# Seven products for more K pairs of a float32 feed-forward, with weight sums on GpSimd

## The chip, the cores and the metric

One core of one Trainium2 chip runs the whole program. The metric is the device time of one execution in microseconds (us), the median of three runs. TensorE (PE) multiplies, VectorE (DVE) and ScalarE (ACT) prepare its operands and read its results, GpSimd (POOL) adds, SyncE (SP) issues the loads.

## The reference, cut to what matters

Two transformer blocks in float32 over 256 tokens of width 2048. Only the matrix products of the two feed-forward networks and the residual around them are touched:

```python
# first block: silu(gate) * up, D_FF = 5632
x = x + (jax.nn.silu(h @ w_gate[l]) * (h @ w_up[l])) @ w_down[l]
# second block: a causal width-3 convolution between the products
u = causal_dwconv(jnp.einsum('bsd,df->bsf', h2, w_up[l]), conv_w[l], conv_b[l])
x = x + jnp.einsum('bsf,fd->bsd', jax.nn.silu(u_gate) * u_val, w_down[l])
```

## The kernel before, in words

**Float32 by three products.** An operand is cut into a high half (float32 rounded to the fp32r type) and a low half (the difference). `split` (L78) does it for weights: ACT casts a loaded tile `raw` into `wh` (L80), DVE subtracts `wh` from `raw` into `wl` (L81). `mm3` (L131) then issues high x high, high x low, low x high, three matmuls of 512 columns into one PSUM bank (L132 to L134). `wh` and `wl` have four buffers of 1024 columns each.

**The large products.** `gemm` (L167) makes 256 tokens x 1024 columns, four PSUM banks, over `nk` K pairs (a pair is 2 x 128 rows of K, one 1 MB load). A plain pair needs 8 `mm3`, that is 24 matmuls. For the first `n_sum` pairs Winograd's form of Strassen's scheme is used: 7 products of sums, 21 matmuls. It needs sums of the activations (`Pair.sums`, four 128-column blocks, made once per pair on POOL at L122 to L125) and sums of the weight blocks, `ta` and `tb`, made on DVE for every tile (L187 to L189). Each such pair has four cuts: 512 columns of `raw`, 1024 of `ta`, 1024 of `raw`, 1024 of `tb`. After the last of them a chain of five operations (L212 to L216) turns the seven sums into corrections `plus`, which are added to the banks at the end (`block` L243, `add_blocks` L253 on POOL and L254 on DVE).

**Where it is called.** FFN1: 11 gate/up gemms with `nk` = 8 ("gates" below), in three parts of 3, 4 and 4; after each part two down gemms (`g` = 0, 1) over 6, 8 and 8 pairs. FFN2: `conv` (L917) makes one 128-row block at a time with the weights as the moving operand; after each part two down gemms over 6, 8 and 8 pairs. Two pairs of each gate and each down are sevens (`N_SUM` = `N_SUMD` = 2). The products of the first block's attention output, of the second block's gates and of its output projection use `gemm` with no seven.

**Order.** The program text gives dependencies and priority; a scheduler that works with its own timing model fixes the order of each engine's queue at compile time, and each engine then runs its queue in that order. Loads go through SP's queue into three `raw` buffers of 2048 columns.

**Between the stages.** The residual and the constants are loaded in the first projections (`consts`, four loads one behind another). Before FFN2 the row norm is finished (`rtok_from` L315, `bcast` L350): sums on DVE, a square root on ACT, a diagonal `dg` on DVE, one matmul by PE (L355), a copy by ACT. The first `conv` stands behind it.

Of the kernel before, what the change touches and what calls it, by code (L numbers as in the profile page):

```python
# [17 lines left out]
P = 128  # L18
# [12 lines left out]
N_SUM = 2  # L31
N_SUMD = 2
TT_BUFS = 1
# [21 lines left out]
def body(ctx: ExitStack, tc: tile.TileContext, xT, xn, gfr, gp, cst, rst, w1, wo1, wgu, wd,  # L55
# [6 lines left out]
    rp = ctx.enter_context(tc.tile_pool(name="rp", bufs=3))  # L62
# [25 lines left out]
    class Pair:  # L88
# [29 lines left out]
        def sums(self, stag, v):  # L118

            f = sx.tile([P, 4, P], F32, tag="sf", name="sf", bufs=2)  # L120
            a11, a12, a21, a22 = v[:, 0, 0:P], v[:, 1, 0:P], v[:, 0, P:S], v[:, 1, P:S]
            pool.tensor_sub(f[:, 0], a21, a22)  # L122
            pool.tensor_sub(f[:, 2], a11, a21)
            pool.tensor_sub(f[:, 1], f[:, 0], a11)
            pool.tensor_add(f[:, 3], a12, f[:, 1])  # L125
            s = sx.tile([P, 2, 4, P], F32R, tag=stag, name=stag)
            act.copy(s[:, 0], f)
            dve.tensor_sub(s[:, 1], f, s[:, 0].bitcast(F32))
            self.s = s
# [10 lines left out]
    def wstat(ps, src, xs, first=True, last=True):  # L140
        raw = raw_tile(src)
        n = 2 * len(xs)
        h = (n + 1) // 2
        for a, b in ((0, h), (h, n)):
            wh, wl = split(raw[:, a * P:b * P], (b - a) * P)
            for k in range(a, b):
                o = (k - a) * P
                mm_w(ps, wh[:, o:o + P], wl[:, o:o + P], xs[k // 2], k % 2,
                     first and k == 0, last and k == n - 1)

    def xstat(src4, xr, pre=(), then=None):
        pp = (bank("d"), bank("d"))
        for q in range(4):
            raw = pre[q] if q < len(pre) else raw_tile(src4[q])
            if then and q in then:
                then[q]()
            for h, kn in ((0, 1), (1, 1), (2, 2)) if pre and q == 0 else ((0, 2), (2, 2)):
                wh, wl = split(raw[:, h * 512:(h + kn) * 512], kn * 512)
# [8 lines left out]
    def gemm(srcs, xs, n_sum, mid=None, tag="d"):  # L167


        nk = len(xs)  # L170
        plus = None
        if n_sum:
            p1, p5, p7 = bank(), bank(), bank()
            c = [[bank("d"), bank("d")], [None, None]]
            p6 = bank()
            c[1] = [bank("d"), bank("d")]
            p2, p3, p4 = c[0][0], c[0][1], c[1][0]
        else:
            c = [[bank(tag), bank(tag)], [bank(tag), bank(tag)]]
        for i in range(n_sum):  # L180
            st, sp_ = i == 0, i == n_sum - 1
            raw = raw_tile(srcs[i])
            b11, b12, b21, b22 = (raw[:, o:o + 512] for o in (0, 512, 1024, 1536))
            ta = sx.tile([P, 2, 512], F32, tag="ta", name="ta", bufs=TT_BUFS)
            tb = sx.tile([P, 2, 512], F32, tag="tb", name="tb", bufs=TT_BUFS)
            b1122 = raw.rearrange("p (a b) -> p a b", b=512)[:, 0:4:3, :]
            dve.tensor_add(ta, b1122, b12.unsqueeze(1).to_broadcast([P, 2, 512]))  # L187
            dve.tensor_add(tb[:, 0], ta[:, 0], b22)
            dve.tensor_add(tb[:, 1], tb[:, 0], b21)  # L189
            pr = xs[i]  # L190
            s = pr.s

            def S_(q):
                return s[:, 0, q], s[:, 1, q]

            def A_(j, t):
                return pr.a(0, j, t), pr.a(1, j, t)

            wh, wl = split(b11, 512)
            mm3(p1, *A_(0, 0), wh[:, 0:512], wl[:, 0:512], st, sp_)  # L200
            wh, wl = split(ta.rearrange("p a b -> p (a b)"), 1024)
            mm3(p5, *S_(0), wh[:, 0:512], wl[:, 0:512], st, sp_)
            mm3(p7, *S_(2), wh[:, 512:1024], wl[:, 512:1024], st, sp_)
            wh, wl = split(raw[:, 1024:2048], 1024)
            mm3(p2, *A_(1, 0), wh[:, 0:512], wl[:, 0:512], st, False)
            mm3(p3, *S_(3), wh[:, 512:1024], wl[:, 512:1024], st, False)
            wh, wl = split(tb.rearrange("p a b -> p (a b)"), 1024)
            mm3(p6, *S_(1), wh[:, 0:512], wl[:, 0:512], st, sp_)
            mm3(p4, *A_(1, 1), wh[:, 512:1024], wl[:, 512:1024], st, False)
        if n_sum:  # L210
# [6 lines left out]
            plus = [[s1, u4], [u3, e22]]  # L217
        for i in range(n_sum, nk):
            raw = raw_tile(srcs[i])
            ws = [split(raw[:, j * 1024:(j + 1) * 1024], 1024) for j in range(2)]  # L220
            order = [(j, t, n) for j in range(2) for t in range(2) for n in range(2)]
            if i == nk - 1:
                order = [(j, t, n) for t in range(2) for n in range(2) for j in range(2)]
            for j, t, n in order:
                wh, wl = ws[j]
                o = n * 512
                mm3(c[t][n], xs[i].a(0, j, t), xs[i].a(1, j, t), wh[:, o:o + 512], wl[:, o:o + 512],
                    i == n_sum and j == 0 and (n_sum == 0 or (t == 1 and n == 1)), i == nk - 1 and j == 1)
            if mid and i == min(n_sum + 1, nk - 1):
                mid()  # L230
        return c, plus

    ET_BUFS = 10
# [32 lines left out]
    def pair_of(srcs, i, tag, gains=None, stag=None, pool_=xp):  # L266
# [8 lines left out]
        else:  # L275
            v = sx.tile([P, 2, S], F32, tag="sv", name="sv", bufs=2)
# [97 lines left out]
    raw0 = rp.tile([P, 2048], F32, tag="raw", name="raw")  # L374
    for a, b in ((0, 1), (1, 2), (2, 4), (4, 8), (8, 12), (12, 16)):
        lo = 0 if a == 0 else 16 + a * S
        nc.sync.dma_start(xin[:, lo:16 + b * S], xT[:, lo:16 + b * S])
        if b <= 4:
            nc.sync.dma_start(raw0[:, a * 512:b * 512], w1[0][0][:, a * 512:b * 512])
# [4 lines left out]
        if b == 4:  # L384
            first.append(raw0)
        elif a in (4, 8):
            first.append(raw_tile(w1[0][a // 4]))
# [10 lines left out]
    with tc.tile_pool(name="a1", bufs=1) as ap1:  # L398
# [13 lines left out]
        def consts():  # L412
            for d, src in ((cst_t, cst), (rst_t, rst), (gp_t, gp), (resid, xn)):
# [117 lines left out]
        for grp in range(4):  # L531
# [38 lines left out]
    sx = sctx.enter_context(tc.tile_pool(name="sx", bufs=max(1, N_SUM)))  # L570
# [12 lines left out]
    for part, (ga, gb) in enumerate(PARTS):  # L583
        n_pairs = 2 * (gb - ga)
        hs = [None] * n_pairs
        for gi in range(ga, gb):
            c, p = gemm(wgu[gi], xr, N_SUM, run_late)
            ht = []
            for t in range(2):
                gt = et("gt")  # L590
                act.activation(gt, block(c, p, t, 0), AF.Silu, scale=rt[:, t:t + 1])
                h = et("h")
                dve.scalar_tensor_tensor(h, block(c, p, t, 1), rt[:, t:t + 1], gt, op0=ALU.mult, op1=ALU.mult)
# [7 lines left out]
        for g in range(2):  # L601
            c, p = gemm([wd[g][2 * ga + i] for i in range(n_pairs)], hs, N_SUMD, run_late)
# [6 lines left out]
    for g, n in enumerate(("ta", "tb")):  # L609
        gf.append(sx.tile([P, 2, 512], F32, tag=n, name="gf", bufs=TT_BUFS))  # L610
# [257 lines left out]
    sx = sctx.enter_context(tc.tile_pool(name="sy", bufs=max(1, N_SUM)))  # L868
    mr = [None] * 8
    ET_BUFS = 6  # L870
    with tc.tile_pool(name="mg", bufs=8) as mp:
        for b in range(4):
            c, p = gemm(wgs[b], xr, 0, run_late)
            gs = [[None, None], [None, None]]
            for t in range(2):
                for n in range(2):
                    gs[t][n] = mp.tile([P, 512], F32, tag="gs", name="gs")
# [28 lines left out]
        for g in range(2):  # L906
            c, p = gemm(wo2[g], mr, N_SUMW, run_late)
# [3 lines left out]
        rt = rtok_from(sq_done(), "rtok", EPS)  # L911
        rb = bcast(rt, "rb")
# [158 lines left out]
```

## Time and profile before

| | |
|---|---|
| median of 3 runs | 2578.12 us (2577.94 to 2578.13) |
| the profiled execution | 2575.72 us, of it the span 2573.8 us |
| mean granted TensorE clock | 0.995 |
| PE busy | 2530.7 us (98%) |
| DVE busy | 1821.8 us (71%) |
| ACT busy | 1340.8 us (52%) |
| POOL busy | 167.3 us (7%) |

The span runs from the first to the last instruction. A matmul's busy time overlaps that of the next one, so the distance between the starts of two matmuls, not the duration of one, says what a matmul costs. A duration of DVE or POOL in these rows runs from the instruction's start to its end, so it holds any time in which it was held up after its start.

### The profile page before, as it was taken

The numbers are of one execution on the slowest core, as the hardware profiler recorded it, in microseconds if no ns is written. First come the engines' busy times: TensorE is split into PE (matmuls) and PEld (weight loads), VectorE is DVE, ScalarE is ACT, GpSimd is POOL, SyncE is SP. The second block draws the span as 40 slices with busy tenths as digits, with TensorE's granted clock in tenths as the row PEclk, the third lists the DMA queues.
The fourth block names the chain that finished last, engine by engine and source line by source line (L and its number), as shares of the span: only waits on it lengthen the run. The fifth ranks groups of instructions, "written<-read, shape, count | busy, mean of one in ns | idle before, by whom it ended". The sixth has DMA issues, their size and how long they took to land. (4 is left out here: it accounts for less than half of the span.)

```text
span 2573.8 us, 31105 instructions
## 1 busy us (share of the span) xinstructions
PE 2530.7 (98%) x12050; PEld 2094.5 (81%) x12050; DVE 1821.8 (71%) x2354; ACT 1340.8 (52%) x1882; POOL 167.3 (7%) x125
## 2 busy tenths in 40 slices
PE   7999999999999999999999999999899999999999
PEld 6888887878878888777888888888788888888887
DVE  6666556789778877877566555455589887878796
ACT  4555555555555454546455644444455455545553
POOL 3000000102101100110000000000000100110011
PEclk9999999999999999999999999999999999999999
DMA  7444444545545555554544455555455655555554
GB/s 273 152 158 170 171 164 158 190 176 198 209 167 210 180 210 170 197 196 165 195 161 154 176 180 188 189 195 180 154 190 180 210 183 185 192 196 184 193 178 166
DMA packets 66244, 472.60 MB, mean 184 GB/s; under 512 B 7345, under 2 KB 7601, under 8 KB 9777
## 3 DMA queue, kind: packets, MB, share of 16 engines
q1 hardware_dynamic: 65520, 468.53, 51.8%
q8 instruction: 94, 1.54, 0.2%
q10 hardware_dynamic: 576, 2.10, 0.2%
q14 instruction: 54, 0.43, 0.0%
HBM read 468.50 MB, written 2.10 MB: 183 GB/s over the span
## 5 line engine op out<-in xcount | busy, mean ns | idle before, releaser
L81 DVE TENSOR_TENSOR wl<-raw,wh 128x1024 fp32r<-128x1024 f32 (+1 forms) x882 | 1082.4, 1234 | 597.3 <-ACT wh L80 596.1
L80 ACT CAST wh<-raw 128x1024 fp32r<-128x1024 f32 (+1 forms) x882 | 902.0, 1029 | 995.1 <-PE d L134 649.5
L133 PE MATMUL d<-wl,x 128*128 128x512 f32 x1532 | 599.6, 393 | 11.6 <-DVE wl L81 11.6
L134 PE MATMUL d<-wh,x 128*128 128x512 f32 x1532 | 597.9, 392 | 0.0
L132 PE MATMUL d<-wh,x 128*128 128x512 f32 x1532 | 572.1, 394 | 3.4 <-ACT wh L80 3.2
L137 PE MATMUL a<-x,wh 128*128 128x512 f32 x1536 | 542.0, 398 | 0.0
L138 PE MATMUL a<-x,wl 128*128 128x256 f32 x1536 | 431.6, 281 | 0.0
L133 PEld LDWEIGHTS d<-wl,x 128*128 128x128 f32 x1532 | 288.4, 188 | 74.8 <-DVE wl L81 15.2
L137 PEld LDWEIGHTS a<-x,wh 128*128 128x128 f32 x1536 | 289.0, 188 | 70.1
L132 PEld LDWEIGHTS d<-wh,x 128*128 128x128 f32 x1532 | 287.1, 188 | 67.1 <-ACT wh L80 8.2
L134 PEld LDWEIGHTS d<-wh,x 128*128 128x128 f32 x1532 | 288.6, 188 | 59.1 <-DVE x L116 0.5
L138 PEld LDWEIGHTS a<-x,wl 128*128 128x128 f32 x1536 | 290.9, 189 | 0.2
L133 PE MATMUL d<-wl,y 128*128 128x512 f32 x624 | 242.2, 391 | 0.0
L134 PE MATMUL d<-wh,y 128*128 128x512 f32 x624 | 241.5, 390 | 0.0
L132 PE MATMUL d<-wh,y 128*128 128x512 f32 x624 | 217.3, 392 | 0.1
L133 PEld LDWEIGHTS d<-wl,y 128*128 128x128 f32 x624 | 117.1, 188 | 27.0 <-DVE wl L81 2.3
L132 PEld LDWEIGHTS d<-wh,y 128*128 128x128 f32 x624 | 116.5, 188 | 25.8 <-ACT wh L80 2.2
L134 PEld LDWEIGHTS d<-wh,y 128*128 128x128 f32 x624 | 117.2, 188 | 24.0
L81 DVE TENSOR_TENSOR wl<-ta,wh 128x1024 fp32r<-128x1024 f32 x46 | 56.2, 1223 | 46.6 <-ACT wh L80 46.6
L132 PE MATMUL a<-wh,y 128*128 128x512 f32 x216 | 83.4, 392 | 3.2 <-DVE x L111 3.2
L134 PE MATMUL a<-wh,y 128*128 128x512 f32 x216 | 84.4, 392 | 0.0
L133 PE MATMUL a<-wl,y 128*128 128x512 f32 x216 | 84.4, 391 | 0.0
(335 smaller groups left out, 2418.9 us busy)
## 6 DMA issues: line engine op xcount, KB each, us to landing
raw<-in_wgu SPq DMA_DIRECT2D x88, 1024.0 KB, 4.8
raw<-in_wd SPq DMA_DIRECT2D x88, 1024.0 KB, 4.8
raw<-in_wup SPq DMA_DIRECT2D x88, 1024.0 KB, 4.8
raw<-in_w SPq DMA_DIRECT2D x47, 1024.0 KB, 4.8
raw<-in_wo SPq DMA_DIRECT2D x32, 1024.0 KB, 4.8
raw<-in_wgs SPq DMA_DIRECT2D x32, 1024.0 KB, 4.8
raw<-in_wfox SPq DMA_DIRECT2D x24, 1024.0 KB, 4.8
raw<-in_wpr SPq DMA_DIRECT2D x16, 1024.0 KB, 4.8
```

Source lines behind the costliest of these rows:

```text
L80: act.copy(wh[:, :n], src)
L81: dve.tensor_sub(wl[:, :n], src, wh[:, :n].bitcast(F32))
L132: pe.matmul(ps, ah, wh, start=start, stop=False)
L133: pe.matmul(ps, ah, wl, start=False, stop=False)
L134: pe.matmul(ps, al, wh, start=False, stop=stop)
L137: pe.matmul(ps, wh, pr.t[:, :, j, :], start=start, stop=False)
L138: pe.matmul(ps[:, 0:S], wl, pr.hi(j), start=False, stop=stop)
```

## The change

- `N_SUM` 2 to 4 (gates: 4 of 8 pairs), `N_SUMD` 2 to 3 (downs).
- The weight sums `ta` and `tb` go from DVE to POOL, the activation sums from POOL to DVE.
- In `gemm` a seven pair alternates with a plain pair as long as there are plain pairs beyond the last `tail` ones (1, in FFN1's downs 2); of such a plain pair the low half of the second tile is subtracted on POOL, too. So a gate has three seven pairs with a plain one, one seven alone and one plain pair behind; an FFN1 down over 6 pairs has one with, two alone and two plain behind; over 8 pairs three with and two plain behind. In FFN2's downs over 6 pairs it is two with, one alone and one plain behind; over 8 pairs three with and two plain behind.
- The four cuts of a seven are 1024 of `raw`, 512 of `raw`, 1024 of `ta`, 1024 of `tb`; `_pairs` lays the four weight blocks out in another order for it.
- `raw` is seven buffers of 1024 columns, each with its own load of 512 KB; `ta` has two buffers, `tb` one.
- The residual's load leaves the constants and comes as two loads at the third attention group. FFN2's row norm is finished behind the first `conv`'s matmuls instead of ahead of them. Some scratch tiles are shared.

```diff
-N_SUM = 2
-N_SUMD = 2
-TT_BUFS = 1
+N_SUM = 4
+N_SUMD = 3
+TA_BUFS = 2
+TB_BUFS = 1
...
-    rp = ctx.enter_context(tc.tile_pool(name="rp", bufs=3))
+    rp = ctx.enter_context(tc.tile_pool(name="rp", bufs=7))
...
-        t = rp.tile([P, 2048], F32, tag="raw", name="raw")
+        t = rp.tile([P, 1024], F32, tag="raw", name="raw")
...
-    def split(src, n):
+    def split(src, n, eng=dve):
         wh, wl = wtiles()
         act.copy(wh[:, :n], src)
-        dve.tensor_sub(wl[:, :n], src, wh[:, :n].bitcast(F32))
+        eng.tensor_sub(wl[:, :n], src, wh[:, :n].bitcast(F32))
...
         def sums(self, stag, v):
-            pool.tensor_sub(f[:, 0], a21, a22)
...
+            dve.tensor_sub(f[:, 0], a21, a22)
+            dve.tensor_sub(f[:, 2], a11, a21)
+            dve.tensor_sub(f[:, 1], f[:, 0], a11)
+            dve.tensor_add(f[:, 3], a12, f[:, 1])
...
+        class Seven:
...
+            def sum_a(self):
+                r = self.r
+                pool.tensor_add(self.ta, r[0].rearrange("p (a b) -> p a b", a=2),
+                                r[1][:, 0:512].unsqueeze(1).to_broadcast([P, 2, 512]))
+            def sum_b(self):
+                pool.tensor_add(self.tb[:, 0], self.ta[:, 0], self.r[0][:, 512:1024])
+                pool.tensor_add(self.tb[:, 1], self.tb[:, 0], self.r[1][:, 512:1024])
...
+        n_with = min(n_sum, max(0, len(plains) - tail))
...
+        for i, sv in enumerate(sevens):
+            pl = plains[i] if i < n_with else None
+            later(sv.load)
+            if pl:
+                later(pl.load)
+            later(sv.sum_a)
+            if pl is None:
+                later(sv.sum_b)
+            sv.one()
+            if pl:
+                later(lambda pl=pl: pl.cut(0, dve))
+                later(lambda pl=pl: pl.cut(1, pool))
+                later(sv.sum_b)
+                pl.part(0)
+            sv.two()
+            if pl:
+                pl.part(1)
+            sv.three()
...
-            for d, src in ((cst_t, cst), (rst_t, rst), (gp_t, gp), (resid, xn)):
+            for d, src in ((cst_t, cst), (rst_t, rst), (gp_t, gp)):
...
+            if grp == 2:
+                for t in range(2):
+                    nc.sync.dma_start(resid[:, t], xn[:, t])
...
-        rt = rtok_from(sq_done(), "rtok", EPS)
-        rb = bcast(rt, "rb")
...
             wstat(ps, wup[n], xr)
+            if not rbs:
+                rbs.append(bcast(rtok_from(sq_done(), "rtok", EPS), "rb"))
```

## Rows read from the trace of the kernel before

**Rows 1.** The page's first part: busy us (share of the span) xinstructions.
```profile
PE 2530.7 (98%) x12050; PEld 2094.5 (81%) x12050; DVE 1821.8 (71%) x2354; ACT 1340.8 (52%) x1882; POOL 167.3 (7%) x125
```

**Rows 2.** Whom PE waited for: us in total, times, longest.
```profile
PE d L133 <- DVE wl L81: 11.6, 5, 8.7
PE a L355 <- DVE dg L353: 7.0, 1, 7.0
```

**Rows 3.** Busy time by stretch: length, engines busy (xinstructions), granted clock, DMA.
```profile
630.00:806.00 176.00, 173.85 (x770) 141.46 (x769) 137.59 (x151) 90.23 (x102) 6.43 (x8) 1.00 0.55 191
564.90:630.00 65.10, 64.59 (x286) 52.12 (x285) 61.83 (x65) 33.42 (x38) 15.65 (x8) 1.00 0.55 194
806.00:893.00 87.00, 86.48 (x382) 70.26 (x381) 72.21 (x73) 41.98 (x46) 15.70 (x8) 1.00 0.55 194
1971.60:2035.90 64.30, 64.07 (x279) 51.61 (x279) 59.31 (x63) 33.59 (x38) 13.98 (x8) 1.00 0.59 205
2216.60:2302.50 85.90, 85.67 (x375) 69.52 (x374) 68.96 (x70) 41.98 (x46) 13.94 (x8) 1.00 0.59 202
2037.00:2216.00 179.00, 179.00 (x1016) 155.12 (x1015) 143.41 (x215) 99.67 (x150) 6.20 (x8) 1.00 0.52 183
```

**Rows 4.** PE in order of time: start us, us, line; first and eleventh.
```profile
640.28 0.39 PE L133 MATMUL d<-wl,x 128*128 128x512 f32 x1
...
642.55 0.39 PE L134 MATMUL d<-wh,x 128*128 128x512 f32 x1
```

**Rows 5.** DVE in order of time, while POOL is idle.
```profile
29.97 2.35 DVE L81 TENSOR_TENSOR wl<-raw,wh 128x1024 fp32r<-128x1024 f32 x2
...
58.26 0.29 DVE L446 TENSOR_TENSOR ro<-nat,rst_t 128x128 f32<-128x128 f32 x1
```

**Rows 6.** Groups of DVE, 475.6 to 1068 us: busy us, mean ns | idle before.
```profile
L188 DVE TENSOR_TENSOR tb<-ta,raw 128x512 f32<-128x512 f32 x28 | 19.3, 688 | 0.4
```

**Rows 7.** POOL in order of time, near the start.
```profile
18.12 2.41 POOL L408 TENSOR_TENSOR sqx<-sqx,sqi 128x1024 f32<-128x1024 f32 x1
20.50 2.07 POOL L407 TENSOR_TENSOR sqi<-xin 128x1024 f32<-128x1024 f32 x1
22.64 3.23 POOL L408 TENSOR_TENSOR sqx<-sqx,sqi 128x1024 f32<-128x1024 f32 x1
```

**Rows 8.** DVE in order of time, the same stretch.
```profile
20.74 6.22 DVE L81 TENSOR_TENSOR wl<-raw,wh 128x1024 fp32r<-128x1024 f32 x2
```

**Rows 9.** POOL in order of time, in an FFN2 down.
```profile
2019.60 3.54 POOL L253 TENSOR_TENSOR xin<-xin,u 128x512 f32<-128x512 f32 x2 [6.97 <-DVE u L214]
2023.10 2.27 POOL L253 TENSOR_TENSOR xin<-xin,e 128x512 f32<-128x512 f32 x1
```

**Rows 10.** DVE in order of time, the same stretch.
```profile
2019.37 0.68 DVE L215 TENSOR_TENSOR u<-a,u 128x512 f32<-128x512 f32 x1
2019.97 2.01 DVE L81 TENSOR_TENSOR wl<-raw,wh 128x1024 fp32r<-128x1024 f32 x1
2021.91 0.68 DVE L216 TENSOR_TENSOR e<-a,u 128x512 f32<-128x512 f32 x1
2022.51 5.08 DVE L81 TENSOR_TENSOR wl<-raw,wh 128x1024 fp32r<-128x1024 f32 x3
```

**Rows 11.** Busy time by stretch, after two long waits of PE (clock third from last).
```profile
17.50:27.60 10.10, 3.90 (x9) 3.13 (x10) 10.10 (x5) 3.03 (x6) 9.86 (x5) 0.51 0.17 71
1833.40:1840.00 6.60, 3.65 (x11) 3.12 (x12) 2.00 (x7) 2.23 (x5) 0.00 (x0) 0.51 0.33 137
```

**Rows 12.** DMA issues: count, KB each, median us to landing; and ACT's casts.
```profile
raw<-in_wgu SPq DMA_DIRECT2D x88, 1024.0 KB, 4.8
L80 ACT CAST wh<-raw 128x1024 fp32r<-128x1024 f32 (+1 forms) x882 | 902.0, 1029 | 995.1 <-PE d L134 649.5
```

More of the change, by code (lines that the diff above doesn't have):

```diff
@@ L153, in xstat @@
         for q in range(4):
-            raw = pre[q] if q < len(pre) else raw_tile(src4[q])
+            raw = pre[q] if q < len(pre) else [raw_tile(src4[q][:, h * 1024:(h + 1) * 1024]) for h in range(2)]
             if then and q in then:
@@ L172, in gemm @@
         if n_sum:
-            p1, p5, p7 = bank(), bank(), bank()
+            p1 = bank()
             c = [[bank("d"), bank("d")], [None, None]]
-            p6 = bank()
+            p5, p7, p6 = bank(), bank(), bank()
             c[1] = [bank("d"), bank("d")]
-            p2, p3, p4 = c[0][0], c[0][1], c[1][0]
         else:
             c = [[bank(tag), bank(tag)], [bank(tag), bank(tag)]]
[L180 to L209, printed above, removed]
@@ L210, in gemm, with mm, go, later @@
-        if n_sum:
+            p1 = p5 = p7 = p6 = None
+        todo, count, done = [], {}, {}
+        def mm(ps, lhs, w, o):
+            count[id(ps)] = count.get(id(ps), 0) + 1
+            def go():
+                k = done[id(ps)] = done.get(id(ps), 0) + 1
+                wh, wl = w[0][:, o:o + 512], w[1][:, o:o + 512]
+                mm3(ps, *lhs(), wh, wl, k == 1, k == count[id(ps)])
+            todo.append(go)
+        def later(f):
+            todo.append(f)
+        class Seven:
+            def __init__(self, i):
+                self.i, self.w = i, [[None, None] for _ in range(4)]
+            def load(self):
+                self.r = [raw_tile(srcs[self.i][:, h * 1024:(h + 1) * 1024]) for h in range(2)]
+                self.ta = sx.tile([P, 2, 512], F32, tag="ta", name="ta", bufs=TA_BUFS)
+                self.tb = sx.tile([P, 2, 512], F32, tag="tb", name="tb", bufs=TB_BUFS)
+            def sum_a(self):
[5 more added lines that the diff above has]
+                pool.tensor_add(self.tb[:, 1], self.tb[:, 0], self.r[1][:, 512:1024])
+            def cut(self, n, src, m):
+                self.w[n][:] = split(src, m)
+            def lhs(self, n):
+                pr = xs[self.i]
+                return (pr.s[:, 0, n], pr.s[:, 1, n]) if n < 4 else (pr.a(0, (n - 4) % 2, (n - 4) // 2),
+                                                                     pr.a(1, (n - 4) % 2, (n - 4) // 2))
+            def one(self):
+                later(lambda: self.cut(0, self.r[0], 1024))
+                mm(p1, lambda: self.lhs(4), self.w[0], 0)
+                mm(c[0][1], lambda: self.lhs(3), self.w[0], 512)
+                later(lambda: self.cut(1, self.r[1][:, 512:1024], 512))
+                mm(c[0][0], lambda: self.lhs(5), self.w[1], 0)
+            def two(self):
+                later(lambda: self.cut(2, self.ta.rearrange("p a b -> p (a b)"), 1024))
+                mm(p5, lambda: self.lhs(0), self.w[2], 0)
+                mm(p7, lambda: self.lhs(2), self.w[2], 512)
+            def three(self):
+                later(lambda: self.cut(3, self.tb.rearrange("p a b -> p (a b)"), 1024))
+                mm(p6, lambda: self.lhs(1), self.w[3], 0)
+                mm(c[1][0], lambda: self.lhs(7), self.w[3], 512)
@@ new lines, in gemm, with __init__, load, lhs @@
+        class Plain:
+            def __init__(self, i):
+                self.i, self.w = i, [[None, None] for _ in range(2)]
+            def load(self):
+                self.r = [raw_tile(srcs[self.i][:, h * 1024:(h + 1) * 1024]) for h in range(2)]
+            def lhs(self, j, t):
+                return xs[self.i].a(0, j, t), xs[self.i].a(1, j, t)
+            def cut(self, h, eng):
+                self.w[h][:] = split(self.r[h], 1024, eng)
+            def part(self, h):
+                for n in range(2):
+                    for t in range(2):
+                        j, col = (n, n) if h == 0 else (n, 1 - n)
+                        mm(c[t][col], lambda j=j, t=t: self.lhs(j, t), self.w[h], n * 512)
+            def by_bank(self):
+                for t, col in LAST:
+                    for h in range(2):
+                        j = col if h == 0 else 1 - col
+                        mm(c[t][col], lambda j=j, t=t: self.lhs(j, t), self.w[h], j * 512)
@@ new lines, in gemm @@
+        sevens = [Seven(i) for i in range(n_sum)]
+        plains = [Plain(i) for i in range(n_sum, nk)]
+        n_with = min(n_sum, max(0, len(plains) - tail))
+        if not n_sum:
+            n_with = 0
+        for i, sv in enumerate(sevens):
[16 more added lines that the diff above has]
+            sv.three()
@@ L216, in gemm @@
             dve.tensor_sub(e22, p5, u3)
[L217 to L233, printed above, removed]
+            return [[s1, u4], [u3, e22]]
+        tails = plains[n_with:]
+        if n_sum:
+            later(lambda: plus_.append(chain()))
+            if mid:
+                later(mid)
+        plus_ = []
+        for i, pl in enumerate(tails):
+            later(pl.load)
+            later(lambda pl=pl: pl.cut(0, dve))
+            later(lambda pl=pl: pl.cut(1, dve))
+            if i == len(tails) - 1:
+                pl.by_bank()
+            else:
+                pl.part(0)
+                pl.part(1)
+            if mid and not n_sum and i == min(1, len(tails) - 2):
+                later(mid)
+        for f in todo:
+            f()
+        return c, plus_[0] if plus_ else None
+    ET_BUFS = 8
     def et(name):
@@ L275, in pair_of @@
         else:
-            v = sx.tile([P, 2, S], F32, tag="sv", name="sv", bufs=2)
+            v = et("sv").rearrange("p (j s) -> p j s", j=2)
             for j in range(2):
@@ L372, in run_late @@
             late.pop(0)()
-    raw0 = rp.tile([P, 2048], F32, tag="raw", name="raw")
+    raw0 = [rp.tile([P, 1024], F32, tag="raw", name="raw") for i in range(2)]
     for a, b in ((0, 1), (1, 2), (2, 4), (4, 8), (8, 12), (12, 16)):
@@ L386, in body @@
         elif a in (4, 8):
-            first.append(raw_tile(w1[0][a // 4]))
+            first.append([raw_tile(w1[0][a // 4][:, h * 1024:(h + 1) * 1024]) for h in range(2)])
     y1 = []
@@ L536, in body @@
                 hb, r2, co, so = 4, 16, R_CA, R_SA
+            if grp == 2:
+                for t in range(2):
+                    nc.sync.dma_start(resid[:, t], xn[:, t])
             if grp > 0:
@@ L601, in body @@
         for g in range(2):
-            c, p = gemm([wd[g][2 * ga + i] for i in range(n_pairs)], hs, N_SUMD, run_late)
+            c, p = gemm([wd[g][2 * ga + i] for i in range(n_pairs)], hs, N_SUMD, run_late, tail=2)
             add_blocks(c, p, g)
```

46 lines of the change are left out of this document (23 added, 23 removed).

## The prediction

> **What bounds the kernel now.** I read the page's first part first: PE is busy 98% of the span, DVE 71%, ACT 52%, POOL 7% [rows 1]. The table of whom PE waited for has only two large entries: 11.6 us for weight low halves, 8.7 of them one wait at the start, and 7.0 us once for `dg`, the norm ahead of FFN2 [rows 2]. So PE sets the time, and almost only its own work counts.
>
> The busy time by stretch then gives each stage's length [rows 3]. Four gates take 176.0 us, 44.0 each; two FFN1 downs over 6 pairs 65.1, over 8 pairs 87.0; FFN2's pairs of downs 64.3 and 85.9; the conv stretch ahead of one 179.0, with DVE busy 143.4 of it.
>
> In PE's order of time, ten steps from matmul to matmul take 642.55 - 640.28 = 2.27 us, 0.227 each [rows 4]. A gate has 2 x 21 + 6 x 24 = 186 such matmuls, 42.2 of its 44.0 us. There is little waiting to win back inside the stages: PE is busy 173.85 of 176.0 us, so at most 0.54 us a gate.
>
> **What the change removes on PE.** Two more sevens in each of 11 gates, one more in each of 12 downs: 34 products, 102 matmuls x 0.227 = 23.2 us. Taken alone that is the gain.
>
> **What POOL and DVE cost each other.** This decides the case, because the change puts POOL to work all through the stages where it was idle (6.43 us in four gates [rows 3]).
>
> With POOL idle, DVE makes two low halves of 1024 columns in 2.35 us [rows 5]. Near the start, with POOL at work, the same two take 6.22, from 20.74 to 26.96 [rows 8]. POOL's operations there explain it to the hundredth [rows 7, 8]: POOL's square ends at 22.57; the first low half ends about 1.09 later, 23.66; POOL's add, started at 22.64, ends at 25.87, which is 2.21 after that; the second low half ends at 26.96, again 1.09 later. Each engine stands still while the other works. The second place is an FFN2 down [rows 9, 10]: a low half started at 2019.97 ends at 2021.98, so POOL's first 512-column add ended 1.09 before, at 2020.89; POOL's next ends at 2023.14, 1.16 after that low half; the three low halves from 2022.51 take 5.08 instead of about 3.5. POOL's part in a turn is 1.14 at the third add (2025.37 less 2024.23). The two chain operations of DVE that read one input from PSUM (L215, L216) keep their 0.68 in the same microseconds. So POOL's adds and those DVE operations whose inputs both lie in SBUF take turns at something they share; I call it the port and count holds of it: DVE 1.09 for 1024 columns, 0.6 for 512 (0.688 alone [rows 6], less the start-up); POOL 2.21 for 1024, 1.14 for 512.
>
> The Trainium skill, "SBUF — State Buffer", Who interferes with whom, speaks against the change: a DVE instruction with two SBUF inputs and a GpSimd instruction that reads SBUF exclude each other for a whole instruction. The trace agrees in both places; by this rule every low half and sum below counts, by the rows the same, so the sum is one.
>
> **The port, stage by stage.** A seven: DVE's four cuts 3 x 1.09 + 0.6 = 3.87, POOL's sums 2.21 + 2 x 1.14 = 4.49; together 8.36, where PE needs 21 x 0.227 = 4.77. A seven with a plain pair: one low half more on DVE and one on POOL, 8.36 + 1.09 + 2.21 = 11.66, where PE needs 45 x 0.227 = 10.2. A plain pair alone: 2.18 against 5.45.
>
> Gate: 3 x 11.66 + 8.36 + 2.18 + two operations with both inputs in SBUF at the end (1.2) = 46.7 us of port. PE has 180 x 0.227 = 40.9 and the transposes. So the port becomes the bound: at best 46.7, if it never idles. With four `wh`/`wl` buffers and one `tb` it can't work far ahead; if it gains nothing during the plain pair behind, a gate is 34.98 + 8.36 + 5.45 + 1.2 = 50.0. Nothing shows which end is nearer, so I take the middle, 48.4. The upper end adds 0.15 for each of 15 POOL operations (the first add took 2020.89 - 2019.60 = 1.29 [rows 9, 10], its hold is 1.14): 52.3.
>
> Activation sums: on DVE, four of 128 columns (0.29 each [rows 5], 0.25 back to back) and two subtractions of 512, 2.2 us of port a pair. FFN1's nine pairs for the downs lie in the gates: 20 us over all. FFN2's nine lie in the convs, where DVE has 179.0 - 143.4 = 35.6 us free [rows 3]: nothing. Those of the first gate lie in the product ahead: nothing, at worst 9 us.
>
> - Gates: 11 x 48.4 + 20 - 11 x 44.0 = +68 (from +50 to +112).
> - FFN1 downs over 6 pairs: 11.66 + 2 x 8.36 + 4.36 + POOL's four residual adds 4.56 = 37.3, or 28.4 + 10.9 = 39.3 with PE's tail uncovered; 38.3 each against 32.55: +11.5 for two.
> - FFN1 downs over 8 pairs: 43.9 or 45.9; 44.9 against 43.5: +5.6 for four.
> - FFN2: the first down of a part finds POOL idle in the convs, so the first sums (6.7 us) are ready. Over 8 pairs 43.9 - 6.7 is under PE's 183 x 0.227 = 41.5; I take 42.3, and 44.9 for the second: 87.2 against 85.9, twice. Over 6 pairs 32 and 38.4 against 64.3. Together +8.7.
>
> **The norm ahead of FFN2.** Its first conv's matmuls now stand ahead of it: 179.0 / 1016 x 32 = 5.6 us [rows 3] of the 7.0 are covered, the rest stays. The granted clock was 0.51 (1.2 GHz) in the stretch behind that wait [rows 11], with 3.65 us of PE work at half speed, 1.8 lost. I take -7 (-5 to -9). Moved with it are a square root on ACT, two multiplications on DVE and L355's matmul; the next conv's casts and low halves queue behind them, with four buffers already full.
>
> **At nothing.** Half-size loads: the same bytes in twice the issues on SP; seven tiles of 512 KB replace three of 1 MB, and a load lands after 4.8 us [rows 12] while half a stage's work is ahead. PE's waits name no DMA; if that cover went, one landing at each of six parts, 29 us; a gain is at most 1. ACT's casts: 16 of about 1 us and four halves a gate [rows 12], 20 of 44 us, off the path. The residual's two loads pass SP at the third attention group, long before its first use in the product behind the fourth; the queue behind them slips by 2 MB at some 190 GB/s, 11 us in all, as it did before in another place: 0.
>
> **Sum.** +68 + 11.5 + 5.6 + 8.7 - 7 = +86.8. The profiled execution took 2575.7 us (span 2573.8, 1.9 around it): 2662.5. The median of the runs was 2.4 above it: 2665. With all lower ends 2635, with all upper ends 2735.
>
> **Rivals.**
> - Side by side: POOL's operations here don't stop DVE's, and PE stays the bound. POOL's own 24.6 us a gate fit into 42. Then 23.2 and 7 are won and about 3 of the gates' waits: 2575.7 - 33.2 + 2.4 = 2545, faster. It decides if the low halves stay at 1.2 us while POOL runs. Against it: rows 7 to 10, with the very instruction. The Trainium skill, "GPSIMD Engine Reference", Engine selection, prices elementwise work on GpSimd at about twice VectorE's time; by that alone it would be this case, and the trace does not agree, since the turns cost DVE, too.
> - A shorter hold: POOL's sums cost 0.34 less per 1024 columns, as the square does beside the add (2.07 to 2.41 [rows 7]). Seven such and eight halves a gate: 3.7 less, 43.0 of port, 44.7 in the middle; downs likewise. 11 x 0.7 + 20 + 2 - 7: +23, 2600. Against it: the square reads one tile twice, the sums read two tiles.
> - The clock falls: the waits for the port grow long enough for a lower granted clock. After the two long waits it was 0.51 over 10.1 and 6.6 us [rows 11]. One stretch of 6.6 us at half speed in each gate loses 3.3, half of that in each down: 36 + 20 on top, 2720. It decides if single waits come near the 7.0 and 8.7 us of rows 2; against it, a seven alone leaves PE only 8.36 - 4.77 = 3.6 us short, in pieces.
>
> **How the numbers follow.** Forecast 0.66, side by side 0.14, shorter hold 0.10, clock 0.10. A measurement of this kernel tells some 0.2% (5 us) from no change. Faster: side by side and a little of the shorter hold, 0.15; within 0.2%: the shorter hold's lower part, 0.03; slower 0.82. The range 2595 to 2735 holds nearly all of the forecast, half of the shorter hold and most of the clock's case, about 0.80.
>
> **What the changed profile would show.** POOL busy some 25 us in each gate by holds alone, its 1024-column adds over 3 us in the mean instead of 2.4; low halves of DVE near 2 us in the gates instead of 1.2; PE waiting for `wl`, for DVE and for POOL, in every seven; a gate at 47 to 52 us; conv stretches as before; the wait at L355 at most 2 us. Wrong if gates are under 44, or if low halves keep 1.2 us beside a busy POOL. If gates are long but PE waits for `raw` or for `wh`, the time is right for another reason.

## The result and the profile after

The changed kernel took 2737.98 us (median of 4 runs, 2733.01 to 2740.21) against 2578.03 before: ratio 1.0618 (95% interval 1.06 to 1.0637), 160 us slower. The forecast was 2665, its range ended at 2735. Direction and mechanism held, the size did not: +87 was forecast. The profiled execution took 2733.01 us, its span 2731.2, the mean granted clock 0.978 (0.995 before).

The page's first part, busy us (share of the span) xinstructions, answers to [rows 1]:

```profile
PE 2577.7 (94%) x11948; PEld 2100.7 (77%) x11948; DVE 2066.4 (76%) x2315; ACT 1403.2 (51%) x1963; POOL 826.1 (30%) x372
```

PE has the 102 matmuls less that the change promised (12050 to 11948). POOL works five times as long as before. DVE has fewer instructions, since the weight sums went to POOL, and is busy 245 us longer all the same: its operations became longer, not more. The table of whom PE waited for (total, times, longest) answers to [rows 2]:

```profile
PE a L134 <- ACT wh L82: 35.9, 15, 3.8
PE a L135 <- DVE wl L83: 28.2, 18, 3.2
PE d L135 <- DVE wl L83: 28.0, 32, 7.4
PE d L134 <- DVE s L329: 19.3, 11, 4.6
PE d L134 <- DVE xin L340: 8.1, 4, 4.1
PE d L135 <- POOL wl L83: 5.0, 7, 0.8
PE a L139 <- DVE x L113: 4.3, 1, 4.3
```

Apart from one of 7.4 us at the start no wait is long; there are very many. The first three entries are cut weights that come late, as forecast. The largest is for `wh`, though, which the prediction had named as the sign of another reason. Here it is not one: 14 of its 15 waits are for the cast of `tb`, and with that cast ACT itself had waited for POOL's sum:

```profile
ACT wh L82 <- POOL tb L213: 78.1, 30, 5.3
```

The fourth and fifth entries were not in the forecast: PE waits for DVE to empty a bank (`s`, `xin`) before a product of the next gemm may write it. By stretch (length; PE, PEld, DVE, ACT, POOL busy; granted clock; DMA share; GB/s), of the kernel before: FFN1 from the evacuation ahead of its first gate to its last one, and FFN2 likewise:

```profile
374.50:1159.20 784.70, 768.83 (x3396) 625.05 (x3395) 618.22 (x668) 403.36 (x476) 71.87 (x56) 0.99 0.54 188
1824.00:2565.60 741.60, 733.94 (x3855) 624.62 (x3853) 597.87 (x808) 401.53 (x560) 61.37 (x48) 1.00 0.53 185
```

The same of the changed kernel, and four stretches inside:

```profile
373.00:1290.40 917.40, 806.44 (x3320) 627.71 (x3319) 815.35 (x630) 455.89 (x543) 586.05 (x257) 0.96 0.48 161
1956.20:2724.70 768.50, 744.43 (x3846) 628.74 (x3845) 645.41 (x807) 411.42 (x575) 205.53 (x94) 0.98 0.53 177
675.30:891.10 215.80, 184.11 (x743) 142.24 (x744) 192.21 (x143) 103.68 (x118) 139.99 (x62) 0.95 0.47 158
590.70:674.30 83.60, 69.18 (x280) 53.71 (x279) 81.44 (x62) 37.44 (x44) 56.87 (x27) 0.94 0.46 151
890.80:980.40 89.60, 86.79 (x375) 68.89 (x374) 84.81 (x63) 46.18 (x51) 74.17 (x31) 1.00 0.57 188
1990.00:2080.00 90.00, 90.00 (x521) 79.38 (x521) 75.01 (x124) 53.45 (x81) 0.00 (x0) 1.00 0.55 189
```

FFN1 grew by 132.7 us, FFN2 by 26.9: that is the whole loss. Lines three to five are the stretches of [rows 3]: the four gates of FFN1's second part take 215.8 us (176.0 before), 54.0 each; from PE's first product of a stage to its first of the next, the two downs over 6 pairs took 83.6 (65.1), the two over 8 pairs 89.6 (86.9). The convs of FFN2 (last line), where POOL is idle, leave PE without a gap, as before.

What fills a gate stands in POOL's order of time (start us, us, engine, line, operation):

```profile
812.62 3.38 POOL L83 TENSOR_TENSOR wl<-raw,wh 128x1024 fp32r<-128x1024 f32 x1
817.77 2.70 POOL L208 TENSOR_TENSOR ta<-raw 128x1024 f32<-128x1024 f32 x1 [1.77 <-DMA raw<-in_wgu]
820.43 2.27 POOL L212 TENSOR_TENSOR tb<-ta,raw 128x512 f32<-128x512 f32 x1
822.79 1.62 POOL L213 TENSOR_TENSOR tb<-tb,raw 128x512 f32<-128x512 f32 x1
```

and in DVE's, over the same stretch:

```profile
813.66 3.42 DVE L83 TENSOR_TENSOR wl<-ta,wh 128x1024 fp32r<-128x1024 f32 x1
817.00 1.21 DVE L83 TENSOR_TENSOR wl<-tb,wh 128x1024 fp32r<-128x1024 f32 x1
818.14 5.12 DVE L83 TENSOR_TENSOR wl<-raw,wh 128x1024 fp32r<-128x1024 f32 x2
823.18 2.30 DVE L83 TENSOR_TENSOR wl<-ta,wh 128x1024 fp32r<-128x1024 f32 x1
```

POOL's low half ends at 816.00; DVE's `wl<-ta`, started at 813.66, ends 1.08 later, 817.08. POOL's first sum ends at 820.47, 2.26 after DVE's `wl<-tb` (818.21); 1.09 for DVE gives 821.56, 1.14 for POOL 822.70, and POOL's second sum ends there, at 822.70. These are the turns of [rows 7 to 10] in the new stages, with the same holds to within 0.05. A hold runs from the start of an operation, or from the end of the other engine's if that is later, to its own end. Gone through in this way, the three gates from 729.8 to 891.1 hold 72.7 us of DVE's turns and 77.1 of POOL's in 161.3: 49.9 a gate, and some 4 a gate in which neither holds the port. The groups of the four gates (busy us, mean ns | idle before) answer to [rows 5] and [rows 6]; 1.2 us was the low half's time with POOL idle:

```profile
L208 POOL TENSOR_TENSOR ta<-raw 128x1024 f32<-128x1024 f32 x17 | 46.2, 2720 | 49.4 <-DMA raw<-in_wgu 31.2 <-DVE wl L83 13.0 <-DMA raw<-in_wd 5.2
L83 POOL TENSOR_TENSOR wl<-raw,wh 128x1024 fp32r<-128x1024 f32 x12 | 35.9, 2990 | 6.7 <-ACT wh L82 6.7
L83 DVE TENSOR_TENSOR wl<-ta,wh 128x1024 fp32r<-128x1024 f32 x16 | 35.0, 2190 | 1.7 <-ACT wh L82 1.7
```

### The profile page after: what moved, and what is told of

Same layout as the page of the kernel before. It is cut to its first block, busy times and chain, and to the rows that moved or that the text cites. A ratio compares the mean times of both kernels' runs of the same rounds, so it can differ in the third digit from the quotient of the medians.

```text
span 2731.2 us, 32667 instructions
## 1 busy us (share of the span) xinstructions
PE 2577.7 (94%) x11948; PEld 2100.7 (77%) x11948; DVE 2066.4 (76%) x2315; ACT 1403.2 (51%) x1963; POOL 826.1 (30%) x372
## 4 chain that ended last, share of the span: by engine, by line
PE 66%; DVE 15%; issue 7%; POOL 6%; DMA 4%; ACT 2%; SPq 0%; DVEq 0%; ACTq 0%; POOLq 0%
PE d L135 12%; PE d L136 12%; PE a L139 12%; PE d L134 12%; DVE wl L83 9%; PE a L140 6%; DMA raw<-in_wgu 3%; PE a L135 2%; PE a L134 2%; PE a L136 2%; POOL ta L208 2%; POOL tb L213 2%; POOL tb L212 1%; ACT wh L82 1%; DMA raw<-in_wd 1%
## 5 line engine op out<-in xcount | busy, mean ns | idle before, releaser
L83 DVE TENSOR_TENSOR wl<-raw,wh 128x1024 fp32r<-128x1024 f32 (+1 forms) x819 | 1153.2, 1417 | 523.8 <-ACT wh L82 522.0
L208 POOL TENSOR_TENSOR ta<-raw 128x1024 f32<-128x1024 f32 x80 | 222.3, 2779 | 1115.3 <-DMA raw<-in_wd 587.6
L136 PE MATMUL d<-wh,x 128*128 128x512 f32 x1400 | 553.2, 396 | 0.0
L134 PE MATMUL d<-wh,x 128*128 128x512 f32 x1400 | 525.2, 400 | 7.6 <-ACT x L112 3.6
L134 PEld LDWEIGHTS d<-wh,x 128*128 128x128 f32 x1400 | 268.7, 192 | 68.2 <-ACT x L112 5.0
L136 PEld LDWEIGHTS d<-wh,x 128*128 128x128 f32 x1400 | 267.2, 191 | 54.4
L136 PE MATMUL d<-wh,y 128*128 128x512 f32 x552 | 215.8, 397 | 3.6 <-DVE y L118 3.6
L83 POOL TENSOR_TENSOR wl<-raw,wh 128x1024 fp32r<-128x1024 f32 x63 | 182.3, 2893 | 81.9 <-ACT wh L82 81.8
L83 DVE TENSOR_TENSOR wl<-ta,wh 128x1024 fp32r<-128x1024 f32 x80 | 180.7, 2259 | 19.9 <-ACT wh L82 19.9
L134 PE MATMUL d<-wh,y 128*128 128x512 f32 x552 | 182.3, 403 | 0.3 <-ACT wh L82 0.3
L212 POOL TENSOR_TENSOR tb<-ta,raw 128x512 f32<-128x512 f32 x80 | 149.8, 1873 | 84.1 <-DVE wl L83 83.4
L83 DVE TENSOR_TENSOR wl<-tb,wh 128x1024 fp32r<-128x1024 f32 x80 | 131.2, 1640 | 33.6 <-ACT wh L82 33.3
L213 POOL TENSOR_TENSOR tb<-tb,raw 128x512 f32<-128x512 f32 x80 | 146.2, 1827 | 5.9
```

Of the source, the lines that this page charges most:

```text
L83: eng.tensor_sub(wl[:, :n], src, wh[:, :n].bitcast(F32))
L134: pe.matmul(ps, ah, wh, start=start, stop=False)
L136: pe.matmul(ps, al, wh, start=False, stop=stop)
L208: pool.tensor_add(self.ta, r[0].rearrange("p (a b) -> p a b", a=2), r[1][:, 0:512].unsqueeze(1).to_broadcast([P, 2, 512]))
L212: pool.tensor_add(self.tb[:, 0], self.ta[:, 0], self.r[0][:, 512:1024])
L213: pool.tensor_add(self.tb[:, 1], self.tb[:, 0], self.r[1][:, 512:1024])
```

## The experiments

Unless another base is named, an edit is made to the changed kernel. "Gate" is the stretch of FFN1's second part over four. Ratios are to the kernel before, which took 2578.9 to 2580.0 us beside them.

**The sums' reads.** POOL keeps its place in the queue and writes the same tiles, but reads nothing for them: the weight sums are left out.

```diff
-                pool.tensor_add(self.ta, r[0].rearrange("p (a b) -> p a b", a=2),
-                                r[1][:, 0:512].unsqueeze(1).to_broadcast([P, 2, 512]))
+                pool.memset(self.ta, 0.5)
...
-                pool.tensor_add(self.tb[:, 0], self.ta[:, 0], self.r[0][:, 512:1024])
-                pool.tensor_add(self.tb[:, 1], self.tb[:, 0], self.r[1][:, 512:1024])
+                pool.memset(self.tb[:, 0], 0.5)
+                pool.memset(self.tb[:, 1], 0.5)
```

> The changed kernel with the three weight sums of each seven on POOL replaced by three memsets of the same tiles on POOL: the sums are left out, POOL still writes as many columns but reads nothing for them. The low halves on POOL stay. Theory 1 (turns over a read port that both use): DVE's low halves of ta and tb fall from 2.2 and 1.6 us to about 1.2 to 1.4, the port has 25 us of DVE and 7 of POOL in a gate, gates 42 to 45, 2555 to 2600. Rival (POOL's writes collide as well): low halves stay near 2 us, gates over 48. Rival (order and buffers): the memsets take less time than the adds, so this also shortens the chain, but the low halves' durations would not change.

2542.54 us, ratio 0.9857 (0.9838 to 0.9877); gate 42.1. The window of this kernel's four gates:

```profile
622.90:791.30 168.40, 168.40 (x745) 137.71 (x744) 133.78 (x143) 103.42 (x118) 63.13 (x61) 1.00 0.61 201
```

The group of DVE's low halves of `raw` (1024 and 512 columns together) in the four gates, of the changed kernel and then of this one, and this one's low halves of `ta`:

```profile
L83 DVE TENSOR_TENSOR wl<-raw,wh 128x1024 fp32r<-128x1024 f32 (+1 forms) x53 | 92.1, 1761 | 10.7 <-ACT wh L82 10.7
L83 DVE TENSOR_TENSOR wl<-raw,wh 128x1024 fp32r<-128x1024 f32 (+1 forms) x53 | 55.5, 1059 | 21.8 <-ACT wh L82 21.1
L83 DVE TENSOR_TENSOR wl<-ta,wh 128x1024 fp32r<-128x1024 f32 x16 | 29.6, 1847 | 12.4 <-ACT wh L82 12.4
```

PE has no gap, and DVE's mean for `raw` falls from 1761 to 1059 ns. I had expected 1.2 to 1.4 us for `ta` as well, and its mean is 1.85: POOL's low halves were left in place and still read. The nine of the sixteen that start while one of these runs take 2.15 to 2.77 us, the other seven 1.22. 195 us lie between this kernel and the changed one. What was taken away are POOL's reads and, with them, what a sum takes longer than a memset and POOL's waits for the loaded tiles that it would have read; the three are not separated here. POOL itself is still busy 63 us in the four gates. The time is that of the "side by side" rival (2545), in part by luck: the other edits of the change give 22 us by themselves (below), which leaves 15 for the sevens. In a gate the saving on PE is there: 42.1 us, and 43.4 with two sevens and POOL idle, where six matmuls cost 1.36.

**No work for POOL, and one half of it alone.** First the low half alone goes to DVE, then sums and low half, then the sums alone.

```diff
-                later(lambda pl=pl: pl.cut(1, pool))
+                later(lambda pl=pl: pl.cut(1, dve))
...
-                pool.tensor_add(self.ta, r[0].rearrange("p (a b) -> p a b", a=2),
+                dve.tensor_add(self.ta, r[0].rearrange("p (a b) -> p a b", a=2),
...
-                pool.tensor_add(self.tb[:, 0], self.ta[:, 0], self.r[0][:, 512:1024])
+                dve.tensor_add(self.tb[:, 0], self.ta[:, 0], self.r[0][:, 512:1024])
...
```

> The changed kernel with one word undone: the second low half of each alternating plain pair is subtracted on DVE instead of POOL. Theory 1 (DVE and POOL take turns, and the sum of their turns is the stage): each of the three turns of a gate shrinks from about 2.2 to 1.1 us, so a gate falls from 54 to about 50.6 us, an 8-pair down by some 3 if it is bound by the turns; in all about 60 us less, 2680. Rival (order and buffers: a chain of waits from tb, which has one buffer, through POOL's queue sets the stage): the low half leaves POOL's queue, so each chain is shorter by its whole 2.9 us as recorded, some 9 us a gate, 2620. Rival (the low half was hidden): 2735.

> The changed kernel with the weight sums and the plain low halves on DVE, all else as changed (4 sevens in gates, 3 in downs, order, half-size tiles, one tb). POOL is left with the residual adds. Theory 1 (turns): nothing to share any more; DVE's own work in a gate is 4 x 6.2 + 3 x 2.2 + 2.2 + 1.2 + some 8 of PSUM operations and activation sums = 43 to 44 us, near PE's 42; gates 43 to 46, in all 2555 to 2600. Rival (order and buffers): gates stay at 50 or more, 2690 to 2740, since no buffer is added. Rival (DVE becomes the bound, since it was 72% busy): gates 48, 2650.

> The changed kernel with the weight sums on DVE and only the plain low halves left on POOL, three of 2.2 us in a gate. With all on DVE the gates took 46.7 and DVE was their bound. If a turn of POOL stops DVE in full, a low half that leaves DVE (1.1) costs it 2.2 of standing still: +1.1 each, gates near 50, 2640 to 2655. If POOL's turns fall into DVE's work on PSUM operands (5 to 6 us a gate), DVE is relieved: gates 44 to 46, 2575 to 2600.

Low half on DVE, sums on POOL: 2696.23 us, 1.0447 (1.043 to 1.0465), gate 53.1. All on DVE: 2608.38, 1.011 (1.0095 to 1.0125), gate 46.4. Sums on DVE, low halves on POOL: 2647.89, 1.0274 (1.0253 to 1.0296), gate 47.6. The window of the second kernel's four gates:

```profile
646.00:831.70 185.70, 175.34 (x744) 134.86 (x744) 168.63 (x202) 103.96 (x119) 1.42 (x1) 1.00 0.55 181
```

130 of the 160 us come from the work on POOL. Without it DVE itself is near its limit, busy 168.6 of 185.7, and the change still loses 30 us, a little more than I had expected (2600 at most). POOL's 63 low halves, three in each gate and the rest in the downs, cost 40 us by themselves against DVE doing them: each holds the port for 2.21 where DVE's holds it for 1.09. DVE, with 63 operations less, is busy 1982.9 us instead of 1961.0 over the whole execution. The time is the one I had expected of the turns, but not by way of the gates, which I had put near 50. In part POOL's low half itself comes late: PE waits for it 18.8 us in five waits. The first result fell short of what I had expected of it: 3.4 us of turns fewer a gate gave 0.9. Counted as above, the port idles 5.5 us a gate in that kernel, against 3.8 in the changed one, so most of the saved turns went into idle port.

**One buffer for `tb`.** So I gave `tb` a second buffer, alone and with the low half on DVE; FFN1's 512-column scratch tiles (`ET_BUFS`) went from eight to six to make room.

```diff
-TB_BUFS = 1
+TB_BUFS = 2
...
-    ET_BUFS = 8
+    ET_BUFS = 6
```

> The changed kernel with two tb buffers instead of one, paid for with six instead of eight scratch buffers of 512 columns. Theory 1 (turns): the port stands still only some 4 us in a gate, so at most that is to be had, and more likely 1 to 2: 2710 to 2735. Rival (order and buffers): POOL's waits for the single tb (67 us over FFN1) and ACT's for the sum (74 us) go, 5 us or more a gate, 2660 to 2680.

> The changed kernel with both earlier single edits together: plain low halves on DVE and two tb buffers (six scratch buffers). A gate's turns are 46.7 - 3.4 + 1.8 for the activation sums = 45.1 us. With the low halves alone moved the gates stayed at 53.2, with the port idle some 13%. If the single tb was what kept them there, gates fall to 47 to 49, 2625 to 2645. If other waits do it (POOL waits for raw tiles, which come free only behind its own sums), they stay at 51 or more, 2675 to 2690.

Alone 2712.15 us, 1.0512 (1.0497 to 1.0528), gate 52.1. Both: 2658.54, 1.0304 (1.0289 to 1.0319), gate 48.6, as expected, though the time lies above my 2645. Single edits gave 26 and 42 us, together 79, more than their sum of 68: that fits the low half ahead of the sums in POOL's queue and the single buffer as two links of the same chain. The port idles 2.6 us a gate with the second buffer and 2.0 with both. With it alone PE's wait for `wh` in products on `a` falls from 35.9 us to 1.5. What POOL waited for in FFN1 (total, times, longest), in the changed kernel:

```profile
POOL ta L208 <- DMA raw<-in_wgu: 76.1, 27, 5.0
POOL tb L212 <- DVE wl L83: 67.1, 26, 5.3
POOL ta L208 <- DVE wl L83: 56.8, 13, 9.6
```

and in the one with both edits:

```profile
POOL ta L208 <- DMA raw<-in_wgu: 124.7, 22, 8.3
POOL tb L212 <- DVE wl L83: 21.1, 10, 5.2
```

The wait of the `tb` sums shrinks to a third, and that of `ta` for a loaded tile grows. The window of this kernel's four gates:

```profile
651.20:845.60 194.40, 178.32 (x742) 136.66 (x741) 183.61 (x154) 102.65 (x118) 109.50 (x51) 0.98 0.53 173
```

That is 48.6 a gate, where the turns by holds make 4 x 8.36 + 4 x 2.18 + 1.2 + 1.8 = 45.2. DVE is busy 183.6 of 194.4.

**Turns below PE's time.** Three sevens in a gate with both edits of the last experiment, and, in the kernel before, its own two sevens with their sums on POOL.

```diff
-N_SUM = 4
+N_SUM = 3
```

```diff
-            dve.tensor_add(ta, b1122, b12.unsqueeze(1).to_broadcast([P, 2, 512]))
-            dve.tensor_add(tb[:, 0], ta[:, 0], b22)
-            dve.tensor_add(tb[:, 1], tb[:, 0], b21)
+            pool.tensor_add(ta, b1122, b12.unsqueeze(1).to_broadcast([P, 2, 512]))
+            pool.tensor_add(tb[:, 0], ta[:, 0], b22)
+            pool.tensor_add(tb[:, 1], tb[:, 0], b21)
```

> As e10, with three sevens in the gates (3 in downs stay). A gate's turns are 3 x 8.36 + 5 x 2.18 + 1.2 + 1.8 = 39.0 us, under PE's 41.5. Only the sum counts: PE is the bound, gates 42.5 to 44, 2570 to 2590. Waits count beside the sum (as the kernel before with POOL sums showed, 26 us slower at a sum of 31): gates 45 to 48, 2600 to 2640. The kernel with the same three sevens and no POOL took 2556.

> The kernel before with its weight sums (two sevens a gemm, old order, one ta and one tb) on POOL instead of DVE, nothing else. Theory 1 in its plain form (only the sum of the turns counts): a gate's turns are 2 x 8.36 + 6 x 2.18 + 1.2 = 31 us, well under PE's 42, so no change: 2575 to 2585. Theory 1 with waits (both sevens stand at a gemm's start, 16.7 us of turns against PE's 9.5, and no plain pair's work between to cover them): up to 5 us in each of 23 gemms, 2620 to 2690. The two differ in whether turns are averaged over a gate.

The first: 2619.98 us, 1.0158 (1.0143 to 1.0173), gate 46.3, where turns make 39 and PE 183 x 0.227 = 41.5. The second: 2605.62, 1.0102 (1.0086 to 1.0117), between the two ranges that I had expected, gate 44.6, where turns make 2 x 8.36 + 6 x 2.18 + 1.2 = 31. Both sums lie under PE's time, and neither kernel has it for free: the sum of turns is a lower bound, and single waits count beside it. In the second kernel PE waits for low halves 21.6 and 18.2 us (in products on `a` and on `d`) where it waited 0.8 and 11.6.

**The other edits.** DVE does everything, with the number of sevens as it was (the edit shown, beside the sums' and the low half's move to DVE), and with one more in the gates (`N_SUM` 3).

```diff
-N_SUM = 4
-N_SUMD = 3
+N_SUM = 2
+N_SUMD = 2
```

> The changed kernel with the old number of sevens (2 and 2) and all weight sums and low halves on DVE: what is left of the change is the alternating order, half-size tiles, activation sums on DVE, the residual's loads and the norm. Theory 1 (turns): POOL idle in the stages, DVE has some 36 us of work in a gate: PE bound, gates 43 to 44.3, with the norm's 2 to 4 us 2565 to 2577. Rival (the new order or the half-size tiles cost by themselves, as through the accumulator banks that the second product of a gemm needs): over 2585.

> As e6, with 3 sevens in the gates (2 in downs). PE saves 3 matmuls a gate, 11 x 0.68 = 7.5 us. Theory 1 with DVE's own work as the next bound: port and PSUM work of DVE 3 x 6.2 + 5 x 2.2 + 9 = 38.5 under PE's 41.5, so PE stays the bound: gates 42.5 to 43.5, 2557 to 2570, faster than the kernel before. Rival (DVE already sets the seven stretches, as it did with 4: 46.7 a gate): 44 to 45 a gate, 2575 to 2590.

With two 2557.68 us, 0.9917 (0.9903 to 0.993), gate 43.4; with three 2556.19, 0.991 (0.9896 to 0.9923), gate 43.2. The intervals overlap, so these two are the same. Either beats both kernels, and by a little more than expected (2565 and 2557 at the least). The gates' window of the first:

```profile
626.90:800.50 173.60, 172.97 (x769) 141.87 (x768) 142.48 (x164) 90.02 (x101) 0.00 (x0) 1.00 0.61 198
```

and of the second:

```profile
629.00:801.60 172.60, 171.14 (x757) 139.35 (x756) 156.20 (x182) 95.91 (x109) 0.00 (x0) 1.00 0.59 197
```

With the two sevens of before, the same sums on DVE and the same number of matmuls, a gate lost 0.6 us here and the eleven gates 12 (478.3 against 490.4, from PE's first product of a stage to its first of the next), though I had priced what is left of the change, the norm apart, at nothing: the order of sevens and plain pairs, the half-size tiles, the activation sums on DVE. Which of them it was is not separated.

**The norm alone**, in the kernel before.

```diff
-        rt = rtok_from(sq_done(), "rtok", EPS)
-        rb = bcast(rt, "rb")
...
             wstat(ps, wup[n], xr)
+            if not rbs:
+                rbs.append(bcast(rtok_from(sq_done(), "rtok", EPS), "rb"))
```

> The kernel before with one part of the change: FFN2's row norm is finished behind the first conv's matmuls. The prediction's step: 5.6 of the 7.0 us wait are covered and 1.8 of half clock, -7 (-5 to -9), 2571. Theory now (what is late next is the last x pair that the first conv multiplies, for which the changed kernel's PE waited 4.3 us at this place): 7.0 - 4.3 and little of the clock, -2 to -4, 2575. Rival (the moved norm delays the second conv as much): 0.

2576.49 us against 2579.28, 0.9988 (0.9979 to 0.9997). The wait of 7.0 us for `dg` [rows 2] is gone from this kernel's table of PE's waits, and this stands in its place:

```profile
PE a L137 <- DVE x L111: 4.3, 1, 4.3
```

The conv that was moved ahead needs its own input, the last cut of `x`, and that is late too. So 7.0 - 4.3 = 2.7 us were won, as the medians say.

## Why the prediction was right and wrong

**Added up.** In medians: other edits -22 (two sevens on DVE against before), two more sevens a gate and one more a down on DVE +51 (2608.38 against 2557.68), the same work on POOL +130; together +159. The saving on PE is inside: the kernel without POOL's reads shows 15 of its 23.2 us against the kernel with two sevens.

**Right.** The mechanism, and the holds to within 0.05. That the port becomes the bound and PE waits in small pieces. POOL busy 35.0 us a gate (25 by holds alone), DVE's low halves 1.76 of `raw` and 2.19 of `ta` (near 2); the convs unchanged. POOL's sum of 1024 columns, at 2.72 in the mean, stayed under the 3 of the forecast. The rival "shorter hold" is out, since the sums hold 2.26 and 1.14. The sentence on the Trainium skill, "GPSIMD Engine Reference", Engine selection, stands as it was put there: about twice VectorE's time is what POOL's operation costs itself. The trace agrees with that, 2.21 us to 1.09. Moving the 63 low halves still cost the kernel 40 us: what POOL took on also stopped DVE.

**Wrong: the gate.** The step that failed is "Nothing shows which end is nearer, so I take the middle, 48.4", with 1.8 for activation sums 50.2; the gates measured 54.0 in the second part. Of the difference, the turns themselves are 49.9 where I had 48.5, and some 4 us are port idle where the middle left 1.7: POOL's queue holds the low half of a plain pair, then `tb` into the one buffer, then the next `ta`, which waits for a tile to be loaded. Nothing gets ahead. Two edits on that chain took 5.4 us off a gate, of which the saved turns make 3.4. So the end without work ahead was the nearer one, not the middle, and even it (50.0 + 1.8) was low. By PE's order of time the gates of the three parts took 164.5, 216.5 and 215.2 us against 138.4, 176.0 and 176.0: +105.8 where +68 stood, 38 of the 70 us by which the profiled execution missed.

**Wrong: a wait that was not in the sum.** A gate ends with operations that empty its banks, and an early product of the next gemm writes into one of them: PE waited 19.3 us for `s` and 8.1 for `xin`, 27.4 over the kernel, inside the gates and downs counted here. These operations stand in DVE's and POOL's queues, and with the queues late they are late, too: with all the work on DVE the two waits are 5.7 and 5.8, and with POOL reading nothing neither stands among PE's six largest.

**Wrong: the downs.** FFN1's two over 6 pairs took 83.6 us (forecast 76.6); its four over 8 pairs took 89.6 and 96.3 against 86.9 and 93.5 before, +5.5 as forecast. FFN2's part of the forecast was +8.7 - 7 = +1.7, and it measured +26.9. Its pairs of downs took 77.4, 95.2 and 95.9 against 64.0, 85.8 and 90.3: +28.4. The second down of each pair came near its forecast (38.7, 46.4 and 44.1 for 38.4 and 44.9); the first took 38.8, 48.8 and 46.7 where I had 32 and 42.3. So the step that failed is that "the first sums (6.7 us) are ready" brings a part's first down back to PE's time. POOL's queue in the first down of a part, whose first product PE starts at 2101.10, by time:

```profile
2082.51 2.40 POOL L208 TENSOR_TENSOR ta<-raw 128x1024 f32<-128x1024 f32 x1 [211.04 <-DMA raw<-in_wd]
2084.99 2.16 POOL L212 TENSOR_TENSOR tb<-ta,raw 128x512 f32<-128x512 f32 x1
2087.22 1.35 POOL L213 TENSOR_TENSOR tb<-tb,raw 128x512 f32<-128x512 f32 x1
2097.17 2.41 POOL L208 TENSOR_TENSOR ta<-raw 128x1024 f32<-128x1024 f32 x1 [8.59 <-DMA raw<-in_wd]
2103.25 2.66 POOL L83 TENSOR_TENSOR wl<-raw,wh 128x1024 fp32r<-128x1024 f32 x1 [3.67 <-ACT wh L82]
2107.57 3.14 POOL L208 TENSOR_TENSOR ta<-raw 128x1024 f32<-128x1024 f32 x1 [1.66 <-DMA raw<-in_wd]
```

The sums were ready, as I had said: one seven's and the next `ta`, which ends at 2099.58. But POOL had stood 8.59 us for that `ta`'s loaded tile: SP's queue, which issues the loads, was itself waiting for DVE's work in the convs (from 2086 to 2098 for low halves 11.0 us in four waits, for `ev` 6.4 in two). Behind the `ta` POOL stands again, for a cast and for the next loaded tile, and PE waits 4.8 us within this down. What came early once was lost at the next sums. The other parts' first downs were not gone through in this way. The norm gave 2.7 of its 7.

**Open.** The clock: in the four gates it was 0.95, a tenth of the stretch at 1.2 GHz, about 21 us, of which PE can have lost half, 2.7 a gate. It is 1.00 with POOL's sums reading nothing and with all work on DVE (0.98 with both edits), so it came with the waits; whether it lay on the path was not separated. Over the whole execution the means of 0.978 and 0.995 make some 120 us at 1.2 GHz against some 26 before, at most 47 us of PE's time. It is the third rival's mechanism, with at most four fifths of the 3.3 that I gave it for a gate; how much of the 160 us it made stays open. Likewise not tried: more `raw` buffers, which the sum's wait of 124.7 us points to.

## What to carry to other kernels

Before work is given to GpSimd, add up, stage by stage, the holds of all its operations that read SBUF and of VectorE's that read two SBUF tiles, because the two take turns; the sum has to lie well below the time of the engine that bounds the stage (with 39 us of turns under 41.5 of TensorE a gate took 46.3, and 43.2 with the same work on VectorE alone). Where both alternate, count as well how far the second engine can run ahead: buffers, and what stands in its queue in front, decide between a sum of holds and a sum of waits. The saving on the bound that put its preparation on two engines with one port was a loss here; the version with three sevens in a gate and all sums on VectorE is 0.9% faster than the kernel before.

## What the runs showed of the hardware that I had not expected

GpSimd writing a tile without reading one (a memset of 1024 columns, 958 ns) did not lengthen VectorE's low halves: in the four gates of the kernel whose sums are left out, 14 of `raw` with 1024 columns and all 16 of `tb` ran beside a memset and took 1.22 us in the mean, as long as those beside an idle GpSimd. And short VectorE operations pay for a whole turn. In VectorE's order of time, in the changed kernel:

```profile
433.87 2.70 DVE L130 TENSOR_TENSOR sx<-sf,sx 128x512 fp32r<-128x512 f32 x1
...
436.56 0.68 DVE L130 TENSOR_TENSOR sx<-sf,sx 128x512 fp32r<-128x512 f32 x1
```

and on GpSimd in the same microseconds:

```profile
433.63 2.38 POOL L208 TENSOR_TENSOR ta<-raw 128x1024 f32<-128x1024 f32 x1 [9.62 <-DVE wl L83]
```

The same operation takes 2.70 us when it starts 0.24 behind GpSimd's sum, which ends at 436.01, and 0.68 when GpSimd has nothing to do.
